# A delta-rule recurrence with one chained product a chunk instead of two, its chunk matrices and read-outs made in batches, and chain steps issued a little later

## The chip, the cores and the metric

The kernel runs on one core of a Trainium2 chip. The time is that of one execution on the device in microseconds (us); smaller is better. The core has a matrix engine (TensorE, PE in the profile; PEld is its loading of the stationary operand), three engines for elementwise work (VectorE = DVE, ScalarE = ACT, GpSimd = POOL) and DMA queues, here issued by SyncE (SP). Each engine works through its own instructions in the order in which they were written, and waits on semaphores for the others.

## The reference

One decoder layer on a sequence of 1024 tokens of width 1024, in float32: RMSNorm and a wide input projection, dilated attention in three groups, an RWKV-7 recurrence, a gated merge, an output projection, a squared-ReLU MLP of width 4096, and a gated per-layer embedding. The change touches the recurrence alone (8 heads of 64 channels):

```python
seq = tuple(jnp.moveaxis(t, 1, 0) for t in (r_h, w_h, k_h, v_h, -kk, kk * a_h))

def step(state, inp):
    r_t, w_t, k_t, v_t, a_t, b_t = inp
    sa = jnp.einsum('bhvk,bhk->bhv', state, a_t)
    state = (state * w_t[:, :, None, :] + sa[..., None] * b_t[:, :, None, :]
             + v_t[..., None] * k_t[:, :, None, :])
    y = jnp.einsum('bhvk,bhk->bhv', state, r_t)
    return state, y

_, y = lax.scan(step, state0, seq)
mean = jnp.mean(y, axis=-1, keepdims=True)
var = jnp.mean(jnp.square(y - mean), axis=-1, keepdims=True)
y = (y - mean) * lax.rsqrt(var + RWKV_GN_EPS)
y = y.reshape(B, S, RWKV_WIDTH) * ln_w + ln_b
bonus = jnp.sum(r_h * k_h * r_k, axis=-1, keepdims=True) * v_h
y = (y + bonus.reshape(B, S, RWKV_WIDTH)) * g
```

## The kernel before

**Dense work.** All large products are made of three fp32r matmuls of 128x128 by 128x512 (high by high, high by low, low by high; `mm3`, lines 253, 255, 257). The input projection writes 48 column blocks of 128 (`z`), each in two halves of 24 matmuls. Twelve of them feed the recurrence, 18 the attention, 16 the gates.

**The recurrence.** The 8 heads are 4 units `w` of two heads; a unit's 1024 tokens are 16 chunks of 64. For each unit:
- `elementwise` makes the decays (cumulative sums `Ep`, one VectorE scan a chunk), the scaled operands `AR` (delta vectors and receptances) and `BK`, and by 64-deep products A for each head the chunk matrices `TM`.
- `invert` inverts the 32 triangular matrices by substitution: 31 steps of two VectorE operations (`pt`, `xy`), then a few transposes and products (`tq`, `tr`) that give `TN`.
- `fold_v` puts the centred values and the products `kv` into `UV`.
- `fold` transposes `BK` (`bt`), and multiplies by the inverse (`fq`), so that `TM` holds folded matrices.
- `scan` walks the 16 chunks: a product q (128x128 by 128) of the state with `AR`; VectorE adds it to `UV`; two products y, one a head, give the new state's terms and the outputs; two VectorE operations make the new state `S`, which the next q needs. So a chunk has two products in its chain.
- `post`, every four chunks, takes the outputs with tokens on partitions, normalises them, transposes (`yt`), adds bonus and gate, and stores to `o_scr`.

**What sets the order.** The program has no fixed order of its matmuls. A planner (`Order`) keeps its own clock `t` with costs for each engine, and holds chains, which are generators, and a list of dense work. `run` resumes the first chain whose due time has come, otherwise it writes the next dense matmul. A chain step is due when the planned end of what it needs has passed, plus a margin: 0.1 in `run`, `until` and `hold` (the last one frees a bank of the accumulator). `Engine.__getattr__` records each vector instruction's planned end; its lines give the L100 that the profile shows for nearly all vector work, as L236 stands for single matmuls (`mm`) and L244 for transposes (`tr`). `invert` runs as a chain of its own (`inverses`), `elementwise` as another (`prepare`), and `fold_v`, `fold`, `scan` as a third (`rwkv`). The attention starts when the last `post` is done; the merge's matmuls, when the attention's last block is.

Of the kernel before, what the change touches and what calls it, by code (L numbers as in the profile page):

```python
# [10 lines left out]
F32 = mybir.dt.float32  # L11
# [24 lines left out]
HOP, HOP_DMA = 0.15, 2.5  # L36
TABLE = {AF.Exp: 0, AF.Sqrt: 1, AF.Sigmoid: 2, AF.Tanh: 2}

C_ID, C_MASK, C_BLK, C_RST, C_EPS, C_GN = 0, 128, 256, 384, 448, 449
N_CS0 = 450  # L40
# [35 lines left out]
class Engine:  # L76
# [3 lines left out]
    def __init__(self, eng, order, fixed, per):  # L80
        self.eng, self.order, self.fixed, self.per = eng, order, fixed, per
        self.end, self.table = 0.0, None

    def __getattr__(self, name):
        f = getattr(self.eng, name)

        def call(*a, **kw):
# [7 lines left out]
            self.end = max(self.end, o.t, *(o.written.since(x, self) for x in ins)) + us  # L95
# [20 lines left out]
class Order:  # L116
# [75 lines left out]
    def until(self, t):  # L192
        return max(t - self.t, 0.0) + 0.1
# [8 lines left out]
    def hold(self, tag):  # L202
        self.busy[tag] = self.dep + 0.1
# [3 lines left out]
def layer(ctx: ExitStack, tc: tile.TileContext, x, pT, wz, wup, w_out, wff1, w_ff2, w_ple, w_pleg,  # L207
# [88 lines left out]
    def zbank():  # L296
        tags = ("z0", "z1", "s0")
        if ("X", 0) in done and ("P", NU - 1, 3) not in done:
            tags = tags[0:2]
# [9 lines left out]
    with tc.tile_pool(name="xin", bufs=1) as xp:  # L309
# [75 lines left out]
        for q in range(4):  # L385
# [12 lines left out]
            "px": 1024, "pg": 512, "ex": 512, "py": 512, "gst": 512}  # L398
# [127 lines left out]
    rst = cs[:, C_RST:C_RST + 64]  # L526
# [7 lines left out]
    SB3 = [const.tile([128, 128], F32, name=f"S{i}") for i in range(3)]  # L534
    for t in SB3:
        V.memset(t, 0.0)
# [6 lines left out]
    def elementwise(w):  # L543
# [40 lines left out]
        AR = rtile([128, NCH, 128], "AR", f"AR{w % 2}")  # L584
        G.tensor_tensor(AR[:, :, 64:128], c3(r), c3(Ep), OP.mult)
        d2 = sch.dep
        yield sch.until(d0)
# [8 lines left out]
        V.scalar_tensor_tensor(AR[:, :, 1:64], c3(kk)[:, :, 1:64], -1.0, c3(Ep)[:, :, 0:63],  # L596
                               op0=OP.mult, op1=OP.mult)
        V.tensor_scalar(AR[:, :, 0], kk[:, 0::64], -1.0, None, op0=OP.mult)
# [3 lines left out]
        TM = rtile([128, 2, NCH, 128], "TM", f"TM{w % 2}")  # L602
        yield sch.until(max(sch.dep, d2))
        for g in range(4):
# [3 lines left out]
            for c in range(4):  # L608
                for h in range(2):
                    hp = slice(64 * h, 64 * h + 64)  # L610
                    mm(pa[h][:, c, :], BK[hp, 4 * g + c, :], AR[hp, 4 * g + c, :], 0.1)
            for h in range(2):
                V.tensor_tensor(TM[:, h, cg, :], pa[h], mask[:, None, :].to_broadcast([128, 4, 128]), OP.mult)
                sch.hold(f"m{h}")
        U[w] = dict(AR=AR, BK=BK, TM=TM, wc=wc)
        V.scalar_tensor_tensor(c3(r), AR[:, :, 64:128], pc(P_RK), BK[:, :, 64:128],
                               op0=OP.mult, op1=OP.mult)
        sch.spawn(bonus(w, r), 2, 2.0)
        done.add(("E", w))

    def bonus(w, r):
# [7 lines left out]
        done.add(("r", w))  # L629

    def invert(w):
        TA = U[w]["TM"][:, :, :, 0:64].rearrange("p h c t -> p (h c) t")
# [5 lines left out]
        for b in range(2):  # L638
            q = slice(32 * b, 32 * b + 32)
            V.transpose(Mp[q], TA[q, :, q].rearrange("s q t -> s t q"))  # L640
            yield max(V.end - 0.4 - sch.t, 0.0)
        for s in range(31):
            n = 31 - s
            pv = pt[:, 0:(s + 1) * n].rearrange("q (t p) -> q t p", t=n)
            V.tensor_tensor(pv, X[:, s:s + 1, 0:s + 1].to_broadcast([64, n, s + 1]),
                            Mp[:, s + 1:, s:s + 1].to_broadcast([64, n, s + 1]), OP.mult)
            V.tensor_tensor(X[:, s + 1:, 0:s + 1], X[:, s + 1:, 0:s + 1], pv, OP.add)
            yield max(V.end - 0.4 - sch.t, 0.0)
# [6 lines left out]
        yield max(V.end - 0.4 - sch.t, 0.0)  # L655
        V.transpose(TA[q2, :, q2].rearrange("p q t -> p t q"), X[q2])
        d1 = V.end
        yield sch.until(d0)
        for b in range(2):
            ps, tag = yield from chain_bank([128, 16, 32], "tq")  # L660
            for i in range(16):
                p = 16 * b + i
                mm(ps[32:64, i, :], TA[0:32, p, 32:64], TN[0:32, p, 0:32], 0.064)
# [1002 lines left out]
```

## Time and profile before

| | |
|---|---|
| median of 3 runs | 1843.86 us (1843.84, 1843.86, 1846.53) |
| profiled execution | 1846.24 us, its span 1844.0 us |
| mean granted TensorE clock | 0.981 |
| large matmuls of the input projection | from 13.4 to 874 us |
| recurrence, first head sum to last output transpose | 80.1 to 584 us |
| attention | 589 to 861 us |
| output projection to the end | 951 to 1837 us |

A group line of the profile gives the line, the engine, the operation, out<-in, shapes (contraction * output rows, then the moving operand) and count, then busy time and mean duration, then the engine's idle time just before such instructions and what ended it. A timeline line gives start, duration and instruction, with the idle time before it in brackets. Matmuls overlap, so what one costs is read from start to start.

### The profile page before, as it was taken

The numbers are of one execution on the slowest core, as the hardware profiler recorded it, in microseconds if no ns is written. First come the engines' busy times: TensorE is split into PE (matmuls) and PEld (weight loads), VectorE is DVE, ScalarE is ACT, GpSimd is POOL, SyncE is SP. The second block draws the span as 40 slices with busy tenths as digits, with TensorE's granted clock in tenths as the row PEclk, the third lists the DMA queues.
The fourth block names the chain that finished last, engine by engine and source line by source line (L and its number), as shares of the span: only waits on it lengthen the run. The fifth ranks groups of instructions, "written<-read, shape, count | busy, mean of one in ns | idle before, by whom it ended". The sixth has DMA issues, their size and how long they took to land.

```text
span 1844.0 us, 24622 instructions
## 1 busy us (share of the span) xinstructions
PE 1768.5 (96%) x9392; PEld 1425.4 (77%) x9392; DVE 1085.1 (59%) x2033; ACT 749.6 (41%) x1358; POOL 766.2 (42%) x507
## 2 busy tenths in 40 slices
PE   9998998899899999999999999999999999999898
PEld 8777777687677777777778788888888888887786
DVE  6375793976844333334852745555555676888454
ACT  5933334333334434345442533333333333334353
POOL 1422223121113233332230166666666798896411
PEclk9998999999999999999999999999999999999999
DMA  4621220221323222232551411111111111112321
GB/s 157 239 72 47 66 75 33 75 74 42 101 89 102 81 58 58 69 89 101 180 170 63 150 58 46 46 58 46 46 69 57 47 46 46 57 47 80 103 78 49
DMA packets 54999, 146.03 MB, mean 79 GB/s; under 512 B 6625, under 2 KB 13281, under 8 KB 54882
## 3 DMA queue, kind: packets, MB, share of 16 engines
q1 hardware_dynamic: 54882, 144.46, 23.6%
q8 instruction: 74, 1.21, 0.3%
q14 instruction: 43, 0.35, 0.1%
HBM read 110.49 MB, written 27.26 MB: 75 GB/s over the span
## 4 chain that ended last, share of the span: by engine, by line
PE 72%; DVE 7%; ACT 2%; issue 2%; DMA 1%; POOL 1%; DVEq 0%; ACTq 0%; SPq 0%; POOLq 0%
PE z L255 15%; PE z L257 15%; PE z L253 15%; PE bk L253 6%; PE bk L255 6%; PE bk L257 6%; DVE xy L100 1%; PE po L236 1%; DVE tot L100 1%; PE sc L236 1%; PE y L236 1%; DVE pt L100 1%; DMA g<-gscr 1%; PE pt L244 1%; PE q L236 1%
## 5 line engine op out<-in xcount | busy, mean ns | idle before, releaser
L100 POOL TENSOR_TENSOR wl<-wr,wh 128x1024 fp32r<-128x1024 f32 (+1 forms) x88 | 211.2, 2400 | 502.9 <-ACT wh L100 502.7
L100 DVE TENSOR_TENSOR tot<-tot,bk 128x512 f32<-128x512 f32 x468 | 308.2, 685 | 189.0 <-PE bk L257 188.3
L253 PE MATMUL z<-uh,wh 128*128 128x512 f32 (+1 forms) x800 | 318.6, 398 | 2.8 <-ACT v L100 1.9
L255 PE MATMUL z<-ul,wh 128*128 128x512 f32 (+1 forms) x800 | 319.3, 399 | 0.3 <-DVE ul L100 0.3
L257 PE MATMUL z<-uh,wl 128*128 128x512 f32 (+1 forms) x800 | 319.4, 399 | 0.2 <-POOL wl L100 0.2
L253 PE MATMUL z<-f,wh 128*128 128x512 f32 x512 | 200.1, 391 | 1.9 <-ACT f L100 1.9
L255 PE MATMUL z<-f,wh 128*128 128x512 f32 x512 | 200.2, 391 | 0.2 <-DVE f L100 0.2
L257 PE MATMUL z<-f,wl 128*128 128x512 f32 x512 | 200.0, 391 | 0.0
L100 ACT ACTIVATE duo<-sum 128x512 fp32r<-128x512 f32 x150 | 90.4, 626 | 226.1 <-PE bk L257 120.3
L253 PEld LDWEIGHTS z<-uh,wh 128*128 128x128 f32 x800 | 152.8, 191 | 31.6 <-issue 3.4
L257 PEld LDWEIGHTS z<-uh,wl 128*128 128x128 f32 x800 | 153.1, 191 | 31.1 <-issue 5.4
L255 PEld LDWEIGHTS z<-ul,wh 128*128 128x128 f32 x800 | 152.9, 191 | 30.3 <-issue 5.3
L100 ACT ACTIVATE wh<-wr 128x1024 fp32r<-128x1024 f32 (+1 forms) x88 | 91.6, 1041 | 183.5 <-PE z L255 165.7
L257 PE MATMUL bk<-duo 128*128 128x512 f32 x420 | 163.5, 389 | 0.0
L255 PE MATMUL bk<-duo 128*128 128x512 f32 x420 | 163.5, 389 | 0.0
L253 PE MATMUL bk<-duo 128*128 128x512 f32 x420 | 163.5, 389 | 0.0
L100 POOL TENSOR_TENSOR duo<-sum,duo 128x512 fp32r<-128x512 f32 x75 | 100.6, 1341 | 102.3 <-ACT duo L100 102.3
L253 PEld LDWEIGHTS z<-f,wh 128*128 128x128 f32 x512 | 96.5, 188 | 22.2 <-ACT f L100 2.1
L255 PEld LDWEIGHTS z<-f,wh 128*128 128x128 f32 x512 | 96.4, 188 | 20.5 <-DVE f L100 0.5
L257 PEld LDWEIGHTS z<-f,wl 128*128 128x128 f32 x512 | 96.5, 189 | 20.0
L100 POOL TENSOR_TENSOR sum<-w2r 128x512 f32<-128x512 f32 x75 | 99.6, 1329 | 7.3 <-DVE oc L100 2.6
L100 POOL TENSOR_TENSOR sum<-hr 128x512 f32<-128x512 f32 x75 | 97.5, 1309 | 4.8 <-DVE duo L100 3.1
(293 smaller groups left out, 3255.0 us busy)
## 6 DMA issues: line engine op xcount, KB each, us to landing
wr<-in_wz_dram SPq DMA_DIRECT2D x48, 512.0 KB, 3.5
w2r<-in_w_ff_dram SPq DMA_DIRECT2D x32, 512.0 KB, 3.5
wr<-in_wff_dram SPq DMA_DIRECT2D x32, 512.0 KB, 3.5
xt<-in_x_dram SPq DMA_DIRECT2D x16, 512.0 KB, 4.4
gscr<-gst SPq DMA_DIRECT2D x32, 256.0 KB, 2.0
g<-gscr SPq DMA_DIRECT2D x16, 512.0 KB, 4.9
sw<-qk SPq DMA_DIRECT2D x48, 128.0 KB, 2.3
sascr<-lst SPq DMA_DIRECT2D x16, 256.0 KB, 3.1
```

The costliest lines, as they stand in the source:

```text
L100: return f(*a, **kw)
L236: PE.matmul(out_, a, b, start=start, stop=stop)
L244: PE.transpose(out_, a, ident if idn is None else idn)
L253: PE.matmul(ps, ah, bh, start=i == 0, stop=False)
L255: PE.matmul(ps, ah, bl, start=False, stop=False)
L257: PE.matmul(ps, al, bh, start=False, stop=i == n - 1)
```

## The change

The chunk's state is now carried as one 128x64 matrix for both heads, in the place of the delta vectors in `AR`, and the recurrence over chunks becomes `state = w * (q + own term)`, with q one product of a chunk matrix and the last state. What was done chunk by chunk moves out of the loop:
- `fold` also transposes the delta vectors (`at`), multiplies `TM` by `UV` for all chunks (`kx`: each chunk's own term), and multiplies the transposed delta vectors by the folded matrices (`wr`), which gives each chunk's transition matrix and its read-out from the incoming state.
- `scan` is one product and one VectorE operation a chunk, for chunks 1 to 14.
- `read_out` makes all outputs in two batches of eight chunks, with channels on partitions.
- `post` works on 512 tokens instead of 256. It takes the variance by a matmul (`hv`), and transposes the factors (`yt`) instead of the outputs.

The layout of `TM` and `AR` is turned to fit, the cumulative sums take two chunks at a time, and in the planner the margin is now `LAG`, 0.4 instead of 0.1. An invert step may be written early, into VectorE's planned idle time before another instruction (`spare`).

```diff
+LEAD, SPARE, LAG = 0.4, 0.5, 0.4
...
-            self.end = max(self.end, o.t, *(o.written.since(x, self) for x in ins)) + us
+            ready = max((o.written.since(x, self) for x in ins), default=0.0)
+            while self.spare and self.end + SPARE < ready:
+                spare, self.spare = self.spare, None
+                dep, t = o.dep, o.t
+                self.spare = spare if next(spare, None) else None
+                o.dep, o.t = dep, t
+            self.end = max(self.end, o.t, ready) + us
...
-                        c[0] = self.dep + 0.1 if d is None else self.t + d
+                        c[0] = self.dep + LAG if d is None else self.t + d
...
     def until(self, t):
-        return max(t - self.t, 0.0) + 0.1
+        return max(t - self.t, 0.0) + LAG
...
     def hold(self, tag):
-        self.busy[tag] = self.dep + 0.1
+        self.busy[tag] = self.dep + LAG
...
-        for c in range(NCH):
-            V.tensor_tensor_scan(Ep[:, c * 64:c * 64 + 64], rst, En[:, c * 64:c * 64 + 64], 0.0,
-                                 op0=OP.mult, op1=OP.add)
+        for c in range(8):
+            c2 = slice(c * 128, c * 128 + 128)
+            V.tensor_tensor_scan(Ep[:, c2], rst, En[:, c2], 0.0, op0=OP.mult, op1=OP.add)
...
-        AR = rtile([128, NCH, 128], "AR", f"AR{w % 2}")
+        AR = rtile([128, 2, NCH, 64], "AR", f"AR{w % 2}")
...
-        TM = rtile([128, 2, NCH, 128], "TM", f"TM{w % 2}")
+        TM = rtile([128, NCH, 2, 2, 64], "TM", f"TM{w % 2}")
...
     def fold(w):
...
+        for b in range(2):
+            ps, tag = yield from chain_bank([128, 4, 128], "at", ("s0", "s1"))
+            for i in range(4):
+                c = 8 * b + 2 * i
+                tr(ps[:, i, :], AR[:, 0, c:c + 2].rearrange("p c t -> p (c t)"), 0.11)
+            for i in range(2):
+                S.activation(BK[0:64, 8 * b + i:8 * b + 8:2, :], ps[64 * i:64 * i + 64], AF.Copy)
+            sch.hold(tag)
...
+        for g in range(2):
+            cg = slice(8 * g, 8 * g + 8)
+            ps, tag = yield from chain_bank([128, 8, 64], "kx", ("s0", "s1"))
+            for i in range(8):
+                for h in range(2):
+                    hp = slice(64 * h, 64 * h + 64)
+                    mm(ps[hp, i, :], TM[:, 8 * g + i, 0, h], UV[:, 8 * g + i, hp], 0.06)
+            V.tensor_tensor(AR[:, 0, cg], ps, wc[:, cg, None].to_broadcast([128, 8, 64]), OP.mult)
+            sch.hold(tag)
+        for g in range(4):
+            cg = slice(4 * g, 4 * g + 4)
+            ps, tag = yield from chain_bank([128, 4, 128], "wr")
+            for i in range(4):
+                for h in range(2):
+                    hp = slice(64 * h, 64 * h + 64)
+                    mm(ps[hp, i, :], BK[0:64, 4 * g + i, hp], TM[0:64, 4 * g + i, :, h], 0.095)
+            for h in range(2):
+                V.scalar_tensor_tensor(TM[:, cg, 0, h], ps[:, :, 0:64], hb[h],
+                                       ident[:, None, 64 * h:64 * h + 64].to_broadcast([128, 4, 64]),
+                                       op0=OP.mult, op1=OP.add)
+            V.tensor_tensor(AR[:, 1, cg], ps[:, :, 64:128], AR[:, 1, cg], OP.add)
             sch.hold(tag)
...
     def scan(w):
...
+        for c in range(1, NCH - 1):
+            if c % 8 == 1:
+                qb, tag = yield from chain_bank([128, 8, 64], "q", ("s0", "s1"))
+            q = qb[:, (c - 1) % 8, :]
+            mm(q, TM[:, c, 0].rearrange("p h k -> p (h k)"), AR[:, 0, c - 1], 0.113)
+            V.scalar_tensor_tensor(AR[:, 0, c], q, wc[:, c:c + 1], AR[:, 0, c], op0=OP.mult, op1=OP.add)
+            sch.hold(tag)
+            yield None
+
+    def read_out(w):
...
+        for b in range(2):
+            ps, tag = yield from chain_bank([128, 8, 64], "y", (("s2",), ("s3",))[b])
+            for i in range(8):
+                for h in range(2):
+                    hp = slice(64 * h, 64 * h + 64)
+                    c = 8 * b + i
+                    mm(ps[hp, i, :], UV[:, c, hp], TM[:, c, 1, h], 0.06, start=i == 0, stop=False)
+            for i in range(8):
+                for h in range(2):
+                    hp = slice(64 * h, 64 * h + 64)
+                    c = 8 * b + i
                     if c:
+                        mm(ps[hp, i, :], AR[hp, 0, c - 1], AR[hp, 1, c], 0.06, start=False, stop=i == 7)
...
+    def post(w, b, ps, tag):
...
+        S.activation(sq, ps, AF.Square)
+        S.activation(yc, ps, AF.Copy)
+        sch.hold(tag)
         yield None
+        ps, tag = yield from chain_bank([128, 512], "hv")
+        for i in range(4):
+            mm(ps[:, 2 * i:2 * i + 2], sq[:, i * 128:(i + 1) * 128], cs[:, C_BLK:C_BLK + 128:64], 0.215)
...
```

The order of TensorE's instructions, in the chunk loop of the last unit, before (q and y are the loop's products, z the dense work; x2 stands for two alike):

```order
L236 MATMUL q<-S_601,AR 128x128
L253 MATMUL z<-uh_123,wh 128x512
L255 MATMUL z<-ul_125,wh 128x512
L257 MATMUL z<-uh_123,wl 128x512
L236 MATMUL y<-UV,TM 128x64 x2
L253 MATMUL z<-uh_123,wh 128x512
L255 MATMUL z<-ul_125,wh 128x512
L257 MATMUL z<-uh_123,wl 128x512
L236 MATMUL q<-S_602,AR 128x128
```

And the same place of the change, where L244 is `mm` and L261, L263, L265 are `mm3`:

```order
L244 MATMUL q<-AR,TM 128x64
L261 MATMUL z<-uh_124,wh 128x512
L263 MATMUL z<-ul_126,wh 128x512
L265 MATMUL z<-uh_124,wl 128x512
L261 MATMUL z<-uh_124,wh 128x512
L244 MATMUL q<-AR,TM 128x64
```

From one q to the next there were six dense matmuls and the y group; now there are four dense matmuls and nothing else.

At the end of the last unit's `fold` TensorE now has, ahead of the first q, the batches kx and wr (before, q followed upon fq at this place):

```order
L244 MATMUL kx<-UV,TM 64x64 x32
L244 MATMUL wr<-TM,BK 64x128 x16
L263 MATMUL z<-ul_126,wh 128x512
L265 MATMUL z<-uh_124,wl 128x512
L261 MATMUL z<-uh_124,wh 128x512
L263 MATMUL z<-ul_126,wh 128x512
L265 MATMUL z<-uh_124,wl 128x512
L244 MATMUL wr<-TM,BK 64x128 x8
L261 MATMUL z<-uh_124,wh 128x512
L244 MATMUL wr<-TM,BK 64x128 x8
L244 MATMUL q<-AR,TM 128x64
```

What came in are the 32 and 32 products of these two batches, with six dense matmuls among them.

On VectorE, in the first unit's chunk loop while the second unit is inverted, there stood before (UV and S are the loop's steps, `pt` and `xy` the invert steps, `BK` belongs to `elementwise`):

```order
L100 SCALAR_TENSOR_TENSOR S_601<-y,wc,sw 64x64 x2
L100 TENSOR_TENSOR pt<-xy,Mp 64x247
L100 TENSOR_TENSOR BK<-BK,k 128x16x64
L100 TENSOR_TENSOR UV<-q,UV 64x128
L100 TENSOR_TENSOR xy<-xy,pt 64x19x13
L100 TENSOR_TENSOR BK<-BK,En 128x16x64
L100 SCALAR_TENSOR_TENSOR S_602<-y,wc,sw 64x64 x2
```

And now (AR is the loop's only step):

```order
L108 SCALAR_TENSOR_TENSOR AR<-q,wc,AR 128x64
L108 TENSOR_TENSOR pt<-xy,Mp 64x112
L108 TENSOR_TENSOR xy<-xy,pt 64x28x4
L108 TENSOR_TENSOR pt<-xy,Mp 64x135
L108 TENSOR_TENSOR xy<-xy,pt 64x27x5
L108 TENSOR_TENSOR pt<-xy,Mp 64x156
L108 TENSOR_TENSOR xy<-xy,pt 64x26x6
L108 TENSOR_TENSOR pt<-xy,Mp 64x175
L108 SCALAR_TENSOR_TENSOR AR<-q,wc,AR 128x64
```

Between two steps of the loop there now stand several invert steps.

More of the change, by code (lines that the diff above doesn't have):

```diff
@@ L82, in __init__ @@
         self.end, self.table = 0.0, None
+        self.spare = None
     def __getattr__(self, name):
@@ L297, in zbank @@
         tags = ("z0", "z1", "s0")
-        if ("X", 0) in done and ("P", NU - 1, 3) not in done:
+        if ("X", 0) in done and ("P", NU - 1, 1) not in done:
             tags = tags[0:2]
@@ L525, in layer @@
     mask = cs[:, C_MASK:C_MASK + 128]
-    rst = cs[:, C_RST:C_RST + 64]
+    rst = cs[:, C_RST:C_RST + 128]
+    hb = [blk[:, 64 * h:64 * h + 1] for h in range(2)]
     def head_sums(src, hs):
@@ L639, in invert, with steps @@
             q = slice(32 * b, 32 * b + 32)
[L640 to L648, printed above, removed]
+            V.transpose(Mp[q].rearrange("q t (c h) -> q t c h", h=2),
+                        TA[q, :, :, q].rearrange("s c h t -> s t c h"))
+            yield max(V.end - LEAD - sch.t, 0.0)
+        def steps():
+            for s in range(31):
+                n = 31 - s
+                pv = pt[:, 0:(s + 1) * n].rearrange("q (t p) -> q t p", t=n)
+                V.tensor_tensor(pv, X[:, s:s + 1, 0:s + 1].to_broadcast([64, n, s + 1]),
+                                Mp[:, s + 1:, s:s + 1].to_broadcast([64, n, s + 1]), OP.mult)
+                V.tensor_tensor(X[:, s + 1:, 0:s + 1], X[:, s + 1:, 0:s + 1], pv, OP.add)
+                yield s < 30
+        V.spare = steps()
+        while V.spare:
+            spare, V.spare = V.spare, None
+            V.spare = spare if next(spare) else None
+            yield max(V.end - LEAD - sch.t, 0.0)
         TN = U[w]["TN"] = rtile([64, 32, 64], "TN", "BT")
@@ L699, in fold_v @@
             sch.hold(tag)
-        yield from wait(lambda: ("r", w) in done and ("lo", 2, w) in done)
+        yield from wait(lambda: ("bv", w) in done and ("lo", 2, w) in done)
         done.add(("v", w))
@@ L780, in post @@
[L780 to L790 removed]
+        S.activation(vc, ps[:, 0:8], AF.Sqrt, bias=cs[:, C_GN:C_GN + 1], scale=1.0 / HD)
@@ L813, in rwkv @@
             yield from scan(w)
+            yield from read_out(w)
     GORD = (2, 1, 0)
@@ L868, in attention @@
     def attention():
-        yield from wait(lambda: ("P", NU - 1, 3) in done)
+        yield from wait(lambda: ("P", NU - 1, 1) in done)
         amask = rtile([128, 384], "amask", "ex")
```

145 lines of the change are left out of this document (58 added, 87 removed).

## The prediction

> **What bounds the kernel now.** I read the page's totals first, to see which engine's queue the time is.
>
> ```profile
> span 1844.0 us, 24622 instructions
> ...
> PE 1768.5 (96%) x9392; PEld 1425.4 (77%) x9392; DVE 1085.1 (59%) x2033; ACT 749.6 (41%) x1358; POOL 766.2 (42%) x507
> ```
>
> TensorE is busy 96% of the span, and no other engine passes 59%. So the time is what TensorE is given to do plus what it loses: 75 us without a matmul, and the time in which its clock is low. The windows view shows where it loses; its columns are the window's length, each engine's busy time (instructions), the granted clock, the DMA share and GB/s.
>
> ```profile
> core 0: us, PE busy (x) PEld busy (x) DVE busy (x) ACT busy (x) POOL busy (x), PEclk, DMA share, GB/s
> 80.00:590.00 510.00, 467.77 (x3213) 371.95 (x3211) 341.56 (x711) 185.68 (x302) 117.90 (x86) 0.95 0.23 74
> 590.00:875.00 285.00, 280.29 (x1565) 209.82 (x1563) 99.72 (x341) 124.14 (x288) 84.07 (x33) 1.00 0.25 75
> ```
>
> The first window is the recurrence (its first head sum starts at 80, its last read-out ends near 584), the second the attention. In the first, TensorE is idle for 510 − 467.8 = **42.2 us**, and the clock of 0.95 costs 0.05 × 510 = **25.5 us**. The attention has 4.7 us of idle time at full clock. Which work waits is in the groups by line and shape for that window (count, busy us, mean ns, idle before and its releaser).
>
> ```profile
> L255 PE MATMUL z<-ul,wh 128*128 128x512 f32 x413 | 170.8, 413 | 0.0
> ...
> L236 PE MATMUL y<-UV,TM 128*128 128x64 f32 x256 | 38.3, 273 | 9.4 <-DVE UV L100 9.4
> L236 PE MATMUL q<-S,AR 128*128 128x128 f32 x128 | 30.1, 318 | 12.7 <-DVE S L100 12.1
> L236 PE MATMUL A<-AR,BK 64*128 64x128 f32 x256 | 23.0, 315 | 6.5 <-DVE TM L100 6.5
> ...
> L236 PE MATMUL tq<-TN,TM 32*32 32x32 f32 x256 | 10.2, 203 | 4.7 <-DVE TN L100 4.7
> ...
> L244 PE MATMUL bc<-cs,kk 128*128 128x128 f32 x32 | 5.2, 315 | 5.1 <-ACT kk L100 5.1
> ```
>
> The two products of the chunk loop wait 22.1 of the 42.2 us, nearly all for VectorE. The large projections (z, some 3 × 413 matmuls) lie between the chain steps and never wait, so the recurrence is bound by TensorE's queue with holes in it, not by the length of its own chain. A shorter chain is worth nothing by itself; what counts is matmul time added or removed, and holes.
>
> **The change part by part.** Prices come from a quiet part of the last unit, TensorE's timeline (start, us, instruction).
>
> ```profile
> 531.62 0.39 PE L255 MATMUL z<-ul,wh 128*128 128x512 f32 x1
> 531.85 0.38 PE L236 MATMUL q<-S,AR 128*128 128x128 f32 x2
> 531.99 0.48 PE L257 MATMUL z<-uh,wl 128*128 128x512 f32 x1
> 532.30 0.39 PE L253 MATMUL z<-uh,wh 128*128 128x512 f32 x1
> 532.53 0.40 PE L255 MATMUL z<-ul,wh 128*128 128x512 f32 x1
> 532.77 0.55 PE L236 MATMUL y<-UV,TM 128*128 128x64 f32 x4
> 533.13 0.48 PE L257 MATMUL z<-uh,wl 128*128 128x512 f32 x1
> 533.45 0.39 PE L253 MATMUL z<-uh,wh 128*128 128x512 f32 x1
> 533.67 0.40 PE L255 MATMUL z<-ul,wh 128*128 128x512 f32 x1
> 534.07 0.49 PE L236 MATMUL q<-S,AR 128*128 128x128 f32 x2
> 534.31 0.47 PE L257 MATMUL z<-uh,wl 128*128 128x512 f32 x1
> 534.63 0.39 PE L253 MATMUL z<-uh,wh 128*128 128x512 f32 x1
> ```
>
> Starts, not durations, price a group. Undisturbed projections start 0.23 apart (532.30 to 532.53), 0.2275 on the mean of many. From 531.62 to 532.30 stand two of them and a ready q: 0.68 − 0.455 = 0.23. A y group costs 0.92 − 0.455 = 0.46. The q at 534.07 had to wait and costs 0.96 − 0.455 = 0.50, although the page counts no idle time before it: a waiting step loses 0.27 that hides in the drain.
>
> *Removed.* The instruction order has 43 q groups and 50 y groups standing alone and 21 and 14 that share another group's entry, for which I take 0.14 and 0.38: 43 × 0.23 + 21 × 0.14 + 50 × 0.46 + 14 × 0.38 = 41.2. The 16 groups of old output transposes (yt) take 0.39 from start to start in the rows below, with an entry and an exit 0.59 alone and about 0.45 shared (an estimate): 5 × 0.59 + 11 × 0.45 = 7.9. Together **−49**.
>
> ```profile
> 397.99 2.08 PE L236 MATMUL kv<-UV,TM 64*64 64x64 f32 x64
> 400.00 0.50 PE L255 MATMUL z<-ul,wh 128*128 128x512 f32 x1
> ...
> 394.73 1.03 PE L244 MATMUL bc<-cs,kk 128*128 128x128 f32 x8
> 395.51 0.48 PE L253 MATMUL z<-uh,wh 128*128 128x512 f32 x1
> ...
> 410.15 0.46 PE L244 MATMUL yt<-cs,xy 64*128 64x64 f32 x4
> 410.54 0.50 PE L253 MATMUL z<-uh,wh 128*128 128x512 f32 x1
> ...
> 520.21 1.97 PE L236 MATMUL fq<-TM,TN 64*64 64x128 f32 x32
> 522.10 0.49 PE L257 MATMUL z<-uh,wl 128*128 128x512 f32 x1
> ...
> 686.50 0.44 PE L236 MATMUL po<-PB,vkb 128*64 128x128 f32 x4
> ...
> 687.31 0.66 PE L236 MATMUL po<-PB,vkb 128*64 128x128 f32 x8
> ...
> 382.02 1.84 PE L236 MATMUL hs<-cs,kk 128*128 128x2 f32 x16
> ```
>
> *Added*, for all four units. In fp32 one product is two instructions (kv: 32 written, 64 here), a transpose is one.
> - The transposes at and yt, 64 × 0.11 (bc, eight in 0.78 to the next start, and an entry) = 7.0.
> - The variances hv, 64 × 1.84/16 = 7.4.
> - wr has the shape of fq, 256 × 1.89/32 (520.21 to 522.10) = 15.1.
> - The new q, 41 alone at 0.23 and 15 shared at 0.14, = 11.5; half the columns gain little, since y with 64 columns takes 0.36 for four.
> - kx and y, 256 + 256, and the y terms from the state, 240, are not in the trace. The nearest row is kv, with the same 64 by 64 output and two heads side by side, 2.01/64 = 0.0314; the bounds are fq's 0.06 and y's 0.09, which has the same contraction of 128. I take kv, since that depth costs po nothing: its eight take 0.22 more than its four, 0.055 each, like fq's with a depth of 64. So 752 × 0.0314 = 23.6.
> - Entries and changes of shape, about 16 × 0.2 + 12 × 0.1 = 4.4.
>
> Together **+69**, so the matmul work grows by **20 us**; with kx and y at fq's price by 35, at y's own by 50.
>
> *Waits.* The old loop waited at 128 points, the new one at 56. The new step is one q and one VectorE instruction:
>
> ```profile
> 532.27 0.28 DVE L100 TENSOR_TENSOR UV<-q,UV 64x128 f32<-64x128 f32 x1 [0.77 <-PE q L236]
> ```
>
> VectorE starts 0.42 after a ready q (531.85 to 532.27) and works 0.28, so the next q could start 0.75 later. In the order of the last unit it comes four projections and a q later, 4 × 0.2275 + 0.23 = 1.14: ready, with 0.4 to spare.  So I take the hidden 0.27 of some 30 waiting q, and 1.6 of y, as gone but for 1: −9. The idle 22.1 falls with the points, to 56/128 of it, and by 0.3 at some ten waits: 6.7. The other 20.1 lose 0.3 at ten waits: 17. New hand-overs in fold and read-out get 3.3. Idle goes from 42.2 to 27: **−15**. The low clock follows the holes; 25.5 × 27/42 = 17: **−8.5**.
>
> *Elsewhere.*
>
> ```profile
> L253 PE MATMUL z<-oah,wh 128*128 128x512 f32 x32 | 12.7, 396 | 2.1 <-ACT oah L100 2.1
> ```
>
> A step issued later costs nothing while projections stand in between. In the new order the attention ends some 180 projections (41 us) before the last one, where it ended about a dozen before; so these stay late-proof, and one wait for the attention's output should go: **−2**. From the output projection on the order differs by one or two matmuls a group; nothing there. VectorE's 16 cumulative sums become 8, ScalarE's copies change shape, and 48 read-out DMAs of 128 KB become 24 of 256 KB: all beside TensorE's queue, which is priced by the waits above. The invert steps that now fill VectorE's gaps are the one thing that others queue behind, and head the rivals.
>
> The sum is 20 − 15 − 9 − 8.5 − 2 = −14.5 against the profiled execution, 1846.24 (span 1844.0 and 2.2 around it). That lies 2.4 above the median 1843.86 of the three runs, two of which agree within 0.02; taken off the median it gives **1829.4**.
>
> **The rivals.** *The holes move on (slower).* VectorE falls behind for a reason that the change leaves alone.
>
> ```profile
> 132.66 2.50 DVE L100 TENSOR_TENSOR pt<-xy,Mp 64x255 f32<-64x255 f32 x1
> ...
> 132.36 2.54 POOL L100 TENSOR_TENSOR wl<-wr,wh 128x1024 fp32r<-128x1024 f32 x1 [3.88 <-ACT wh L100]
> ...
> 154.88 3.58 PE L236 MATMUL tq<-TN,TM 32*32 32x32 f32 x64 [4.71 <-DVE TN L100]
> ```
>
> An invert step that takes about 0.42 elsewhere took 2.50, to the end of a GpSimd subtraction; then tq waited 4.71, and its 64 took 3.58, where kv's larger 64 took 2.08. If such delays simply come out at the next step that needs VectorE, idle time stays at 42 and the clock at 0.95: 20 − 9 − 2 = +9, **1853**. It decides where idle in the window stays above some 36 us. For it: invert keeps VectorE full, and gaps are now filled with more of it. Against: the quiet unit's slack of 0.4 a step. [...]
>
> *Batches not side by side.* kx and y at fq's price, +15, and the state terms one after another, doubled, +7.5: +8, **1852**. For it: the state terms of two heads lie on different rows of the array and write one bank, where A writes two (pa, one for each head). Against: po for the first part, and kv's pairs, which share a bank. [...]
>
> *The later issue does not suffice.* Each new q still waits a hidden 0.27: 56 × 0.27 = 15, **1844**, no change. The spare 0.4 speaks against it.
>
> *Holes and clock go.* Idle falls to 15, all 10 hidden us go, the clock costs 7: 20 − 27 − 10 − 18.5 − 2 = −37, **1806**. For it: the attention shows that a chain with slack loses little. Against: A, bc and tq keep their reasons.
>
> **How the numbers follow.** Forecast 0.54 (own range 1820 to 1839), holes go 0.17, holes move on 0.14, batches 0.07, later issue 0.08. Faster is most of the forecast, the fourth and a half-strength batch case: 0.70. Within 0.2% (3.7 us, about what a measurement of this kernel can tell from no change): 0.11. Slower: 0.19. The range, 1811 to 1853, reaches to the slower cases' prices and leaves out the lowest end.
>
> **What would show it.** In the window of the recurrence: q with 112 instructions and under 5 us of idle; kx and y at about 0.03 from start to start; idle near 27 and clock near 0.97; tq still waiting for TN. Wrong: starts of 0.06 or more in kx or y, idle of 40, a q cost of 0.50 throughout, or a wait after 1060 that is not there now.

## The result, and the profile after

The changed kernel took 1865.86 us (median of 4, 1861.31 to 1869.03), the kernel before 1845.19 beside it (4 runs, 1843.84 to 1847.34). The ratio is 1.0109, 95% interval 1.0082 to 1.0136: **1.1% slower**, where 1829.4 was forecast, in a range of 1811 to 1853. The profiled execution took 1861.31, with a span of 1859.5.

From the page of the changed kernel, and its windows (columns as in the prediction; the last row ends where the first transposes of the output stage, tp<-cs,hh, start):

```profile
span 1859.5 us, 25870 instructions
...
PE 1788.3 (96%) x10192; PEld 1448.6 (78%) x10192; DVE 1049.0 (56%) x1866; ACT 725.3 (39%) x1300; POOL 770.1 (41%) x507
```

```profile
80.00:590.00 510.00, 466.69 (x3944) 374.19 (x3942) 316.67 (x604) 167.07 (x274) 112.66 (x83) 0.92 0.21 67
590.00:875.00 285.00, 280.66 (x1525) 210.95 (x1524) 102.14 (x305) 116.86 (x256) 92.51 (x36) 1.00 0.28 85
...
80.00:1023.90 943.90, 896.08 (x6121) 707.94 (x6120) 481.97 (x997) 335.92 (x610) 237.57 (x134) 0.96 0.26 82
```

The same stretch of the kernel before:

```profile
80.00:1008.10 928.10, 876.71 (x5316) 685.31 (x5315) 515.58 (x1151) 358.50 (x664) 232.78 (x133) 0.97 0.26 84
```

Behind that point both kernels take 836 us (835.9 and 835.6), so the loss lies ahead of it: 943.9 against 928.1. I split this stretch into three. *Idle* is length minus TensorE's busy time. *Clock loss* is an estimate: half of the time in which TensorE worked while its granted clock was 0.5 (from the trace's records of that clock; in the changed kernel projections start 0.43 apart there, at 266.08 and 266.51, and 0.23 at full clock, at 256.65 and 256.88). The *rest* is matmul work at full clock, with the hidden waits.

| | length | idle | clock loss | rest |
|---|---|---|---|---|
| before | 928.1 | 51.4 | 26.0 | 850.8 |
| after | 943.9 | 47.8 | 34.7 | 861.4 |
| difference | +15.8 | −3.6 | +8.7 | +10.6 |

The rest grew as forecast (20 − 9 = 11). What did not come is the fall of idle time and clock loss. The groups of the changed kernel, in 80 to 590, show where TensorE stands now (L244 is `mm`, L252 `tr`):

```profile
L244 PE MATMUL q<-AR,TM 128*128 128x64 f32 x112 | 21.5, 275 | 8.1 <-DVE AR L108 8.1
...
L252 PE MATMUL bc<-cs,kk 128*128 128x128 f32 x32 | 6.6, 355 | 18.1 <-ACT kk L108 15.7 <-DVE UV L108 2.4
```

q and y waited 22.1 us before; q now waits 8.1 and y not at all. But bc went from 5.1 to 18.1, nearly all in one hole. TensorE's timeline there, and behind it VectorE's and ScalarE's:

```profile
144.53 1.95 PE L244 MATMUL hs<-cs,kk 128*128 128x2 f32 x16 [0.79 <-ACT kk L108]
...
166.60 0.69 PE L252 MATMUL bc<-cs,kk 128*128 128x128 f32 x2 [15.21 <-ACT kk L108]
```

```profile
158.80 1.89 DVE L108 STREAM_TRANSPOSE TM<-xy 32x1024 f32<-32x1024 f32 x1
...
161.97 0.17 DVE L108 TENSOR_SCALAR rn<-hs 128x16 f32<-128x16 f32 x1
162.18 2.17 DVE L108 STREAM_TRANSPOSE TN<-xy 32x1024 f32<-32x1024 f32 x1
162.18 0.22 ACT L108 ACTIVATE rn<-rn 128x16 f32<-128x16 f32 x1 [15.25 <-DVE rn L108]
164.38 1.28 DVE L108 SCALAR_TENSOR_TENSOR a<-AR,pr,BK 128x1024 f32<-128x1024 f32 x1
165.58 0.25 DVE L108 RECIPROCAL rn<-rn 128x16 f32<-128x16 f32 x1
165.92 1.15 ACT L108 ACTIVATE kk<-rn 128x512 f32<-128x512 f32 x2 [3.52 <-DVE rn L108]
```

The second unit's hs ends at 146.5, but its reader on VectorE, rn, runs at 161.97: it stands in VectorE's queue behind the rest of the first unit's inversion. The planner meant that inversion to be done by then: it put bc 21 matmuls, some 5 us, behind hs. The inversion was late. VectorE and then GpSimd of the changed kernel some 30 us earlier show why:

```profile
127.19 0.39 DVE L108 TENSOR_TENSOR pt<-xy,Mp 64x231 f32<-64x231 f32 x1
127.62 2.49 DVE L108 TENSOR_TENSOR xy<-xy,pt 64x231 f32<-64x231 f32 x1
130.14 1.33 DVE L108 TENSOR_TENSOR pt<-xy,Mp 64x240 f32<-64x240 f32 x1
131.50 2.48 DVE L108 TENSOR_TENSOR xy<-xy,pt 64x240 f32<-64x240 f32 x1
134.02 2.49 DVE L108 TENSOR_TENSOR pt<-xy,Mp 64x247 f32<-64x247 f32 x1
```

```profile
121.23 1.17 POOL L108 TENSOR_TENSOR r<-part,r 128x511 f32<-128x511 f32 x1
127.37 2.48 POOL L108 TENSOR_TENSOR BK<-a,En 128x1024 f32<-128x1024 f32 x1 [4.97 <-DMA a<-sascr]
...
130.12 1.09 POOL L108 TENSOR_TENSOR r<-part,r 128x511 f32<-128x511 f32 x1
131.29 2.43 POOL L108 TENSOR_TENSOR AR<-r,Ep 128x1024 f32<-128x1024 f32 x1
133.69 2.55 POOL L108 TENSOR_TENSOR wl<-wr,wh 128x1024 fp32r<-128x1024 f32 x1
```

A step of 0.4 takes up to 2.5; the four lengthened ones in these rows end 0.26 or 0.27 behind the GpSimd instruction beside them (127.62 + 2.49 against 127.37 + 2.48 for the first). As *lateness* I add up, for each VectorE instruction that took over 0.3 us more than the shortest of its kind in the trace, what it took more; each of them from 80 to 590, 26 before and 29 after, lies beside a GpSimd instruction. From 80 to 590 it is 35.6 us before and 43.0 after; in the first inversion 5.8 and 12.9. In the kernel before, neither product of the next unit on GpSimd met the first inversion, whose steps start from 119.7 to 152.3. BK<-a,En ran ahead of it, r's additions and AR<-r,Ep behind it:

```profile
99.43 2.36 POOL L100 TENSOR_TENSOR BK<-a,En 128x1024 f32<-128x1024 f32 x1 [2.96 <-ACT En L100]
...
159.69 1.08 POOL L100 TENSOR_TENSOR r<-part,r 128x511 f32<-128x511 f32 x1
...
178.52 2.38 POOL L100 TENSOR_TENSOR AR<-r,Ep 128x1024 f32<-128x1024 f32 x1
```

This is a part of the change that the shortened diff above doesn't show: the bonus product now goes to `a` and no longer to r. So r of a unit counts as free (`done.add(("r", w))`) as soon as AR is made, and not only after the bonus, and the next unit's r is projected some 38 us earlier (the addition of its first half at 121.23 instead of 159.69). The buffer of `a`, in turn, is free only when the bonus is stored (121.27), so the next unit's `a` is loaded some 41 us later (issued at 123.88 instead of 82.69). That moves BK<-a,En from 99.43 to 127.37. Both moves bring a product into the inversion.

### The profile page after: what moved, and what is told of

Same layout as the page of the kernel before. It is cut to its first block, busy times and chain, and to the rows that moved or that the text cites. A ratio compares the mean times of both kernels' runs of the same rounds, so it can differ in the third digit from the quotient of the medians.

```text
span 1859.5 us, 25870 instructions
## 1 busy us (share of the span) xinstructions
PE 1788.3 (96%) x10192; PEld 1448.6 (78%) x10192; DVE 1049.0 (56%) x1866; ACT 725.3 (39%) x1300; POOL 770.1 (41%) x507
## 4 chain that ended last, share of the span: by engine, by line
PE 75%; DVE 4%; ACT 2%; issue 1%; DMA 1%; POOL 0%; SPq 0%; DVEq 0%; ACTq 0%; POOLq 0%
PE z L261 16%; PE z L263 16%; PE z L265 16%; PE bk L261 6%; PE bk L263 6%; PE bk L265 6%; PE po L244 1%; PE sc L244 1%; PE pt L252 1%; DVE tot L108 1%; PE tp L252 1%; DMA oscr<-yc 0%; PE y L244 0%; DVE pt L108 0%; PE wr L244 0%
## 5 line engine op out<-in xcount | busy, mean ns | idle before, releaser
L263 PE MATMUL z<-ul,wh 128*128 128x512 f32 (+1 forms) x800 | 323.0, 404 | 0.3 <-DVE ul L108 0.3
L261 PE MATMUL z<-uh,wh 128*128 128x512 f32 (+1 forms) x800 | 322.6, 403 | 0.6 <-ACT uh L108 0.6
L265 PE MATMUL z<-uh,wl 128*128 128x512 f32 (+1 forms) x800 | 320.4, 401 | 0.2 <-POOL wl L108 0.2
L261 PE MATMUL z<-f,wh 128*128 128x512 f32 x512 | 200.3, 391 | 1.9 <-ACT f L108 1.9
L263 PE MATMUL z<-f,wh 128*128 128x512 f32 x512 | 200.4, 391 | 0.0
L265 PE MATMUL z<-f,wl 128*128 128x512 f32 x512 | 200.0, 391 | 0.0
L263 PEld LDWEIGHTS z<-ul,wh 128*128 128x128 f32 x800 | 155.2, 194 | 34.6 <-issue 8.1
L261 PEld LDWEIGHTS z<-uh,wh 128*128 128x128 f32 x800 | 155.3, 194 | 33.2 <-issue 6.0
L265 PEld LDWEIGHTS z<-uh,wl 128*128 128x128 f32 x800 | 155.4, 194 | 29.3 <-issue 2.8
L261 PE MATMUL bk<-duo 128*128 128x512 f32 x420 | 163.4, 389 | 0.0
L263 PE MATMUL bk<-duo 128*128 128x512 f32 x420 | 163.4, 389 | 0.0
L265 PE MATMUL bk<-duo 128*128 128x512 f32 x420 | 163.4, 389 | 0.0
L261 PEld LDWEIGHTS z<-f,wh 128*128 128x128 f32 x512 | 96.7, 189 | 22.2 <-ACT f L108 2.1
L263 PEld LDWEIGHTS z<-f,wh 128*128 128x128 f32 x512 | 96.7, 189 | 20.5 <-DVE f L108 0.4
L265 PEld LDWEIGHTS z<-f,wl 128*128 128x128 f32 x512 | 96.7, 189 | 20.0
```

The lines of the kernel that those rows point to most:

```text
L261: PE.matmul(ps, ah, bh, start=i == 0, stop=False)
L263: PE.matmul(ps, ah, bl, start=False, stop=False)
L265: PE.matmul(ps, al, bh, start=False, stop=i == n - 1)
```

## The experiments

Theories: **early r** (the hole and the lateness come from r's release), **locks** (VectorE's steps beside GpSimd's instructions take up to 2.5 us instead of 0.4, which the planner doesn't know; the word names these longer steps, no mechanism is shown), **later issue** (the margin costs), **spare** (invert steps stand in front of others). Idle, clock loss, rest and lateness are of each profiled execution, in the stretches named above.

| run | median us | ratio to before, 95% | profiled | idle | clock loss | rest | lateness | largest gap by 170 |
|---|---|---|---|---|---|---|---|---|
| before, margin 0.1 | 1845.2 | | 1846.2 | 51.4 | 26.0 | 850.8 | 35.6 | tq 4.7 |
| after, margin 0.4 | 1865.9 | 1.0082 to 1.0136 | 1861.3 | 47.8 | 34.7 | 861.4 | 43.0 | bc 15.2 |
| r_late | 1841.7 | 0.9974 to 0.9996 | 1847.4 | 46.0 | 22.9 | 860.7 | 38.7 | tq 8.1 |
| gate_hs | 1855.1 | 1.0042 to 1.0076 | 1851.3 | 51.4 | 22.6 | 860.4 | 40.9 | tq 6.6 + 6.6 |
| lag_00 | 1869.5 | 1.0113 to 1.0146 | 1873.1 | 57.6 | 40.3 | 856.3 | 46.6 | bc 10.7 |
| lag_01 | 1841.0 | 0.9967 to 0.9989 | 1838.7 | 39.3 | 19.9 | 862.0 | 41.3 | bc 12.1 |
| lag_025 | 1866.5 | 1.0098 to 1.0128 | 1865.5 | 48.4 | 38.0 | 860.1 | 43.3 | bc 11.9 |
| lag_06 | 1859.0 | 1.0047 to 1.0087 | 1858.4 | 50.1 | 28.2 | 862.8 | 50.1 | bc 10.8 |
| before_lag | 1867.2 | 1.0100 to 1.0137 | 1862.7 | 63.6 | 33.1 | 847.1 | 33.4 | tq 5.7 |
| r_late_lag_01 | 1848.5 | 1.0011 to 1.0043 | 1850.5 | 41.5 | 30.0 | 860.2 | 29.6 | tq 7.0 |
| no_spare | 1863.8 | 1.0080 to 1.0111 | 1860.7 | 56.0 | 25.4 | 861.6 | 42.9 | bc 15.7 |
| no_sub | 1844.7 | 0.9981 to 1.0001 | 1835.7 | 41.9 | 13.2 | 863.3 | 23.0 | bc 12.1 |
| no_sub_025 | 1842.7 | 0.9972 to 0.9993 | 1840.0 | 39.7 | 19.3 | 862.1 | 25.6 | bc 10.4 |
| no_sub_01 | 1828.9 | 0.9896 to 0.9923 | 1825.9 | 33.2 | 14.2 | 861.1 | 24.2 | bc 10.7 |
| r_late_told | 1848.5 | 1.0005 to 1.0026 | 1850.3 | 48.3 | 20.8 | 862.6 | 32.7 | bc 8.7 |
| r_late_wl_dve | 1843.4 | 0.9977 to 0.9999 | 1843.2 | 43.8 | 20.1 | 860.6 | 13.3 | tq 3.6 |
| r_late_wl_dve_01 | 1837.4 | 0.9941 to 0.9966 | 1835.3 | 41.2 | 12.1 | 862.7 | 15.4 | tq 2.4 |
| r_late_wl_dve_025 | **1818.1** | 0.9841 to 0.9871 | 1818.1 | 28.5 | 12.4 | 859.7 | 13.6 | tq 2.6 |
| r_late_025 | 1825.6 | 0.9874 to 0.9907 | 1825.5 | 29.9 | 17.4 | 859.7 | 32.2 | tq 6.7 |
| before_wl_dve | 1876.9 | 1.0148 to 1.0184 | 1878.2 | 65.8 | 40.5 | 852.6 | 10.6 | none |

**r set free late** (r_late), and **hs held back** (gate_hs):

```diff
     def elementwise(w):
...
-        done.add(("r", w))
         yield sch.until(d0)
...
     def bonus(w, r):
...
+        done.add(("r", w))
         done.add(("bv", w))
```

```diff
+        yield from wait(lambda: w == 0 or ("I", w - 1) in done)
         ps, tag = yield from chain_bank([128, 512], "hs")
...
             yield max(V.end - LEAD - sch.t, 0.0)
+        done.add(("I", w))
         TN = U[w]["TN"] = rtile([64, 32, 64], "TN", "BT")
```

> The changed kernel, but r of a unit counts as free only after its bonus, as before the change, so that the next unit's r is projected and its elementwise work starts later. Lock theory (r set free early puts GpSimd's products BK<-a,En and AR<-r,Ep beside the first inversion, VectorE falls 12.9 us behind instead of 6.9, and the next unit's bc waits 15.2): no hole above 6 before 200 us, idle time 80 to 590 at 32 to 36 instead of 43.3, total 1849 to 1856. Later-issue theory (the margin of 0.4 costs) and more-work theory (the added matmuls are the loss, the hole is paid anyway further on): 1860 to 1866, idle unchanged.

> The changed kernel, but a unit's hs and all behind it (GpSimd's two products too) wait until the inversion steps of the unit before are issued; r is still set free early. Lock theory: the hole of 15.2 shrinks to what the remaining GpSimd subtractions leave, 4 to 8 us, now before tq; total 1850 to 1857. If the hole came from r's projection itself or from the later issue: 1860 to 1866.

r_late gave back 24 us by the medians, more than expected. Its profiled execution, the slowest of its ten, is 13.9 below that of the changed kernel, 11.8 of it clock loss; the hole only shrank to 8.1, now before tq, and the idle time from 80 to 590 only to 39.2, where 32 to 36 was expected. The text above puts both GpSimd products down to r, and only AR<-r,Ep went (to 168.07): BK<-a,En still runs at 126.76, because `a` is as late as in the changed kernel. The first inversion is 9.2 late, against 12.9 in the changed kernel and 5.8 (not 6.9) in the kernel before. No run undoes the half that `a` brings. gate_hs met its total, but not for its reason: GpSimd's two products ran at 127 and 131 as in the changed kernel although hs was held back, the lateness of the first inversion stayed at 11.9, and 13.2 us of gaps came before tq.

**The margin**, in the changed kernel (`LAG` 0, 0.1, 0.25, 0.6 instead of 0.4), in the kernel before (0.4 instead of 0.1), and with late r:

```diff
-LEAD, SPARE, LAG = 0.4, 0.5, 0.4
+LEAD, SPARE, LAG = 0.4, 0.5, 0.1
```

> The changed kernel with the margin of 0.1 us instead of 0.4: the later issue undone alone. Lock theory: bc of the second unit still stands 20 matmuls behind its hs, so the hole of some 15 stays, and waiting steps lose a little more: 1860 to 1875. Later-issue theory: 1843 to 1853.

> The kernel before with the margin of 0.4 instead of 0.1: the later issue alone. My prediction priced the later issue at a few us of gain in hidden waits. Idle time 80 to 590 falls from 42.2 to 32 to 38, but the old loop of 64 steps gets longer and the attention now ends behind the last projection: 1840 to 1850. Later-issue theory: over 1852.

> The changed kernel with no margin at all. Price theory (every step issued later costs in proportion; 0.3 us of margin cost 25 us, so 83 us for each us): about 1833. Coincidence theory (a margin only shifts which units' steps meet on VectorE; the matmul work and hidden waits stay at 861 us between 80 and the first transposes of the output stage, and idle and clock differ): anywhere from 1836 to 1866, with the hole of 11 to 15 us before 170 in it still.

> The changed kernel with a margin of 0.25, between the two measured. Price theory: 1853, half way. Coincidence theory: one of the two ends rather than the middle, or outside them; the first hole is still there.

> The changed kernel with a margin of 0.6. Price theory: 1882, since 0.2 more cost 17. Coincidence theory: no slower than 1866 by rule; the gaps of over 1.4 us between 340 and 500 that 0.4 had (before bc, A, fq, tq) are other ones.

> The changed kernel with r set free late and the margin of 0.1. If the two edits remove different losses of the changed kernel (one the first hole of 15, the other the losses of 340 to 500): about 1861 - 14 - 22, 1823 to 1830. If r set free late only helped by shifting the later units as the margin does: 1835 to 1845, the first hole shorter (5 to 9 before tq), but no further gain from 340 to 500 over either alone.

The first two alone would have proved the later issue guilty: undone it gave back 25 us, added to the kernel before it cost 22. In the kernel before the loss has a place, and it isn't the recurrence's window: there the idle time fell from 42.2 to 39.0, but behind 590 it rose from 9.2 to 24.6 and the clock loss from 3.4 to 12.9. The old loop got longer (its last yt at 610 instead of 584), the last attention product came at 872, behind the last projection at 848 (before, 847 and 874), and the merge's first matmul waited 6.3 for a weight.

The next three refute a price: 1869, 1841, 1866, 1866, 1859 for 0, 0.1, 0.25, 0.4, 0.6 has no order, and the rest stays at 856 to 863 throughout. A margin writes another order, and these orders lose between 59 (lag_01) and 98 us (lag_00) of idle time and clock. With late r 0.1 is worse than 0.4, and its 1848.5 lies above both expected ranges. So lag_01 was one lucky order, while the kernel of the change stands third of the five. lag_01 has the hole too (12.1), so the hole alone doesn't set the time. Late r instead of early r came to +7.5, −41 and −24 us at the margins 0.1, 0.25 and 0.4 (r_late_025 stands below): a gain in two orders of three.

**No early invert steps** (the `while` over `spare` never runs):

> The changed kernel without the inversion steps put into VectorE's planned gaps: the third part of the change undone alone. If those steps stand in the way of others: below 1850, with idle time below 38 between 80 and the output stage. Coincidence theory: idle plus clock loss anywhere between 60 and 95 us instead of 82, total 1840 to 1872; the first hole (hs and bc of the second unit stand in the same rows of the order) stays at 10 to 15.

No gain in this order: idle time rose by 8, clock loss fell by 9. The theory isn't borne out.

**GpSimd's subtractions taken away** (a constant stands for the low part of the weights), TensorE's order unchanged row by row:

```diff
-        G.tensor_tensor(lo[:, :n], raw[:, :n], hi[:, :n], OP.subtract)
+        G.memset(lo[:, :n].bitcast(F32), 1e-4)
```

> The changed kernel, its order on TensorE the same row by row, but in the projections of the recurrence and the attention GpSimd fills wl with a constant instead of subtracting (the low part of the weights is left out). Lock theory: VectorE's instructions beside these subtractions lose their 13.5 us between 80 and 590, of it some 5 us in the first inversion, so the first hole goes from 15.2 to about 10, and with the clock that follows the total falls by 8 to 15, to 1848 to 1857. If GpSimd is not what makes VectorE late: hole of 15, 1861 to 1868.

> The run lag_025 (1866.5) with GpSimd's subtractions replaced by a fill, as in no_sub; TensorE's order is that of lag_025 row by row. If the spread between the margins (1841 at 0.1, 1866.5 at 0.25, 1866 at 0.4) comes from where the subtractions fall on VectorE's steps: 1838 to 1848, within 8 of no_sub (1844.7) and of no_sub_01. If it comes from VectorE's own steps meeting one another: it keeps its distance of some 25 from no_sub_01, 1845 to 1856.

> The run lag_01 (1841.0) with the fill, TensorE's order that of lag_01 row by row. If the spread between the margins comes from the subtractions, lag_01 has few of them in its way: 1833 to 1841. If it comes from VectorE's own steps: it falls by as much as the others, to 1820 to 1831.

At equal orders 21, 24 and 12 us came back by the medians (no_sub's profiled execution is its fastest of eleven): GpSimd's subtractions are shown as a cause, and they cost the two slower orders more. They explain about half of the spread: 0.1 and 0.25 now lie 14 apart instead of 25.5. The fill is also shorter (0.96 against 2.5), so these runs don't tell steps lengthened by the subtractions from a GpSimd that is free sooner. In no_sub the invert steps beside the fill run at their own pace (GpSimd, then VectorE):

```profile
136.64 0.96 POOL L108 MEMSET wl<- 128x1024 f32 x1 [2.75 <-PE z L265]
```

```profile
136.44 0.42 DVE L108 TENSOR_TENSOR xy<-xy,pt 64x256 f32<-64x256 f32 x1
136.89 0.42 DVE L108 TENSOR_TENSOR pt<-xy,Mp 64x255 f32<-64x255 f32 x1
137.34 0.42 DVE L108 TENSOR_TENSOR xy<-xy,pt 64x255 f32<-64x255 f32 x1
```

The step that runs wholly beside this fill takes 0.42 (136.89); beside the subtraction at 133.69 in the changed kernel one took 2.49 (134.02). The first hole barely shrank (15.2 to 12.1): 8.7 of the 12.9 of lateness in the first inversion stayed, beside the next unit's products and additions, and rn still stands behind the inversion.

**The planner told of the lateness** (`V.end += 0.3` behind each invert step, with late r):

> r set free late and margin 0.4 as in the run r_late (1841.7), and the planner charges each inversion step 0.3 us more, as the measured lateness of 9 to 13 us over 31 steps; nothing else is changed. If the first hole is the planner not knowing of VectorE's lateness: the hole of 8.1 before tq shrinks below 2 and the clock episode of 17 us behind it with it, idle plus clock loss 69 to 57, total 1828 to 1836. If such lateness comes out at another step: 1838 to 1850.

The rival was right: tq no longer waits there, but bc then waits 8.7, at 168.9, and the kernel is 7 us slower than r_late.

**VectorE subtracts for itself** in the recurrence, with late r, at three margins; the best of them without it; and the same alone in the kernel before:

```diff
-        G.tensor_tensor(lo[:, :n], raw[:, :n], hi[:, :n], OP.subtract)
+        eng.tensor_tensor(lo[:, :n], raw[:, :n], hi[:, :n], OP.subtract)
...
-        sch.add(body, lambda: wload(wz[wi]), gate)
+        sch.add(body, lambda: wload(wz[wi], eng=G if ("P", NU - 1, 1) in done else V), gate)
```

> r_late with the subtraction wl of the recurrence's projections on VectorE instead of GpSimd. Lock theory: the lateness beside wl (19.8 of 38.7 us in r_late) goes, against about 37 us more work on VectorE (some 31 at 1.2), which the planner knows of; the first hole falls below 5; total 1832 to 1843. If VectorE's queue is then too full: 1848 to 1865, with gaps that VectorE releases in the place of the ones that are gone.

> r_late_wl_dve with the margin 0.1, the candidate for a better kernel. That run's recurrence lost 30 us in idle time and clock against 63 in the kernel before, but its attention ended behind the last projection and lost 13 there (a gap of 8.2 before bk<-orw). Here the last attention product stands some 107 rows ahead of the last projection. If only that tail was in the way: 1824 to 1834. If a new order brings new meetings: 1834 to 1848.

> The same with the margin 0.25 (the last attention product 153 rows ahead of the last projection). With most of the locks gone the margin should matter little: within 8 of r_late_wl_dve_01, 1824 to 1836. If the margin decides by itself as it did with the locks: more than 12 apart.

> r_late_wl_dve_025 (1818.1) with the subtraction back on GpSimd: r set free late and margin 0.25 alone. If VectorE doing its own subtractions is what makes that kernel fast: idle plus clock loss between 80 and the output stage goes from 41 back to 65 to 80 and the total to 1842 to 1857. If the margin and the late r do it: 1818 to 1828.

> The kernel before with the recurrence's subtractions on VectorE, nothing of the change in it. VectorE's lateness beside GpSimd falls from 35.6 to about 15; but the old loop ends late, and the last attention product already stands behind the last projection, so that some 10 us of tail come: 1835 to 1848. If the locks were the whole matter and the change itself worth nothing: 1818 to 1828, as r_late_wl_dve_025.

Against late r alone this is worth 11 us at 0.1, 7.5 at 0.25 and nothing at 0.4, where the attention ends too late and the merge's first matmul waits 8.2. The margin still decides: 0.1 and 0.25 are 19 us apart, where under 8 was expected. The best of the orders tried, r_late_wl_dve_025, is 1.4% faster than the kernel before; the windows:

```profile
80.00:590.00 510.00, 485.52 (x4127) 392.75 (x4127) 318.69 (x632) 175.38 (x281) 70.31 (x62) 0.97 0.23 75
80.00:980.60 900.60, 872.12 (x6112) 690.04 (x6111) 478.55 (x1020) 335.28 (x606) 179.48 (x107) 0.98 0.27 85
```

Idle time of 24.5 at a clock of 0.97 in the first window is what was forecast (27 and 0.97), but with three edits more than the change. r_late_025, which still subtracts on GpSimd, missed its first range of 1842 to 1857 by 16 on the good side, and its rival (1818 to 1828) was right: late r and the margin 0.25 are 20 us ahead of the kernel before by themselves, and the subtractions add 7.5. And the kernel before lost 31 us by the same edit, though its lateness fell to 10.6 and its idle time from 80 to 590 to 32.1. The loss lies behind, with 33.7 of idle time there instead of 9.2: its recurrence ends at 647 instead of 584, and the attention behind the last projection. TensorE waits there for a weight:

```profile
892.25 0.80 PE L253 MATMUL bk<-orw,wh 128*128 128x512 f32 x1 [6.20 <-ACT wh L100]
```

So VectorE's extra work was bearable with the new loop and not with the old one, in the one order tried. That the new loop's single VectorE step a chunk is the reason is argued, not shown.

## Why the prediction was wrong

In the stretch of the table −14.5 was forecast and +15.7 came. Of the 30.2 between them idle time is 13.4 and the clock 17.2; the matmul work with the hidden waits is 0.4 off the other way.

- *Matmul work +20, hidden waits −9:* right as a sum, 10.6 against 11, and the rest stays within 856 to 863 in all 17 kernels with the new loop (847 to 853 in the three with the old). "Batches not side by side" fell: kx, y and the state terms run as kv does. TensorE's timeline of a q and a read-out:

```profile
236.84 0.40 PE L265 MATMUL z<-uh,wl 128*128 128x512 f32 x1
237.08 0.33 PE L244 MATMUL q<-AR,TM 128*128 128x64 f32 x2
237.22 0.48 PE L261 MATMUL z<-uh,wh 128*128 128x512 f32 x1
237.53 0.39 PE L263 MATMUL z<-ul,wh 128*128 128x512 f32 x1
...
238.32 1.15 PE L244 MATMUL y<-TM,UV 128*64 128x64 f32 x32
239.40 1.03 PE L244 MATMUL y<-AR 64*64 64x64 f32 x28
240.36 1.15 PE L244 MATMUL y<-TM,UV 128*64 128x64 f32 x32
```

  32 in 1.08 and 28 in 0.96, both 0.034 each with the entry, the 28 too, which are two heads on different rows that write one bank; kx takes 2.02 for 64 (at 193.4), 0.032 each. The q costs 0.69 − 0.455 = 0.23, the price of a ready one. Of 38 places at full clock where a q stands alone between projections, 30 cost 0.22 to 0.24; before, 10 of 41 did. So the hidden waits went as forecast.
- *Elsewhere −2:* right in kind. The gaps before z<-oah (2.1) and bk<-orw (2.1) are gone, and with them 3.4 of clock loss that the forecast left out.
- *Idle −15:* **this step failed.** It let the 22.1 us at q and y fall with the number of waits to 6.7, which q's 8.1 roughly bears out, and took 20.3 for all the others (17 of the old 20.1, and 3.3 new). Those came to 43.3 − 8.1 = 35.2, with 15.2 in the one hole. The rival "the holes move on" had the right form (idle in the window 43.3, where it said 42), but it let VectorE fall behind "for a reason that the change leaves alone". The change did not leave it alone: with the bonus product in `a`, AR<-r,Ep and r's additions came earlier and BK<-a,En later, all into the first inversion, and lateness there went from 5.8 to 12.9. So the step took as given that VectorE would be ready when the planner said. Beside GpSimd it came late (43.0 us from 80 to 590), and at equal orders 12 to 24 us hung on GpSimd's subtractions.
- *Clock −8.5:* **failed in sign**, +8.7 (22.6 to 34.7 from 80 to 590, 3.4 to nothing behind). The granted clock of the first window was 0.92, where 0.97 was forecast. I let the clock follow the sum of idle time (and 25.5 × 27/42 is 16.4, not the 17 I took, which changes nothing here). It went with the number of low stretches instead: 11, not 8, in the table's stretch, on less idle time. In no_spare 8 stretches cost 25.4 on 56.0 of idle time.
- *The margin:* I priced it by what it spares one waiting step (0.27). In the new loop its effect is to write another order, and the five measured orders differ by 28 us; in the old one it also made the chain longer. A range of −18 to +24 around one forecast didn't allow for that.
- "Later issue does not suffice" (1844) needed each new q to cost 0.50. Most cost 0.23, so it falls.

What stays open: which steps meet in an unlucky order once the subtractions are gone (14 us between the margins 0.1 and 0.25), what `a` in its old place would give back, and what the change would give on the mean of many orders. Matmul work with hidden waits is 6 to 12 us dearer with the new loop in all of them; with late r and nothing else, two of the three margins tried make up for it (1841.7 and 1825.6) and one does not (1848.5).

## What to carry to other kernels

Where a planner writes the order, a change of one constant is a new order: try several values before you give a constant a price, and never settle on two points. Look for what an edit releases early or late, not only for what it computes: one product written to another buffer brought one GpSimd product earlier and another later, both beside a busy VectorE. And price holes together with the low clock that came with them here: 34.7 us of clock loss with 47.8 of idle time in the changed kernel.

## What the runs showed of the hardware

In the kernels before and after, the stretches at half clock lasted 3.41, 6.83, 10.24, 13.65 or 17.07 us, but for the last (6.56 and 6.05), with which the record ends. In the changed kernel eight of the eleven ahead of the output stage began within gaps or up to 1.9 us behind them; the longest of these gaps were 1.4 to 2.5 us, and 15.2 in the hole. Three did not: those at 84.0 and 261.5, without any gap, and at 541.4, behind one of 0.4. Windows of 4 us around the second of them (columns as above), and TensorE's timeline ahead of it:

```profile
256.00:260.00 4.00, 4.00 (x27) 3.53 (x25) 2.09 (x6) 1.73 (x3) 0.00 (x0) 1.00 0.35 105
260.00:264.00 4.00, 4.00 (x21) 3.42 (x22) 2.02 (x6) 1.88 (x5) 0.00 (x0) 0.68 0.06 26
264.00:268.00 4.00, 4.00 (x11) 3.13 (x11) 3.70 (x9) 1.27 (x3) 0.00 (x0) 0.50 0.26 72
```

```profile
258.49 1.84 PE L244 MATMUL hs<-cs,kk 128*128 128x2 f32 x16
...
260.99 1.25 PE L244 MATMUL hv<-cs,sq 128*128 128x2 f32 x8
```

TensorE counts as busy throughout, but 1.84 and 1.25 us of it are matmuls with two columns. Such matmuls stand ahead of the other two as well (hs at 81.14, hv at 538.59 and 540.29). Whether they bring on the low clock is not isolated: hs at 144.53, behind a gap of 0.79, was followed by none before the hole, and the four hs<-cs,kk of the kernel before (80.10, 180.40, 276.21, 382.02) by none within 4.5 us of their start. Nor did the length of a gap decide alone: during one of 2.44 us, from 368.39, the clock went to half at 370.69, and one of 2.12, from 393.37, was followed by no low clock before 425.31.
